# An encoder block: Conv B computed in a third Strassen section of the gate stage, and attention re-paced around a smaller filler

## The chip, the cores and the metric

The kernel runs on one core of one Trainium2 chip. The metric is the device time of one execution in microseconds. The engines are named as in the profile: PE (TensorE, matmuls), DVE (VectorE), ACT (ScalarE), POOL (GpSimd), and SP, which issues most DMAs.

## The reference

One layer, sequence length T = 1024, model width D = 1024, 16 heads of 64, batch 1, everything float32:

```python
h = rmsnorm(x, ln1_g) * (1 + sc1) + sh1          # sc, sh, g from silu(c) @ ada_w + ada_b
q, k, v, cb, cc, cx, ga, gb = split(h @ w_in)    # eight 1024 x 1024 projections
q, k = rmsnorm per head
y_a = stick_breaking_attention(q, k, v)          # 128-query blocks, strictly causal:
      # z = q.k / 8;  a[t,s] = sigmoid(z[t,s]) * prod over s<j<t of (1 - sigmoid(z[t,j]))
y_b = cb * causal_dwconv3(cc * cx)
merged = sigmoid(ga) * (y_a @ w_branch_a) + sigmoid(gb) * (y_b @ w_branch_b)
x = x + g1 * (merged @ w_out)
h = rmsnorm(x, ln2_g) * (1 + sc2) + sh2
x = x + g2 * ((silu(h @ w_ffn_gate) * (h @ w_ffn_up)) @ w_ffn_down)
```

"Conv B" is the projection cb. The change touches it, the attention, and the way to `y_a @ w_branch_a`.

## The kernel before

**Numbers.** Each float32 operand of a matmul is split into a high part, rounded to the fast matmul format by ScalarE (`AF.Copy`), and a low part, the difference, which VectorE computes. A product of two operands takes three matmuls: high by high, high by low, low by high.

**Stages in order of time.** (1) Norm of x, and projections of k and the first half of v. (2) The gate stage: q, Conv C, Conv x and the two branch gates. (3) Attention, with other matmuls as filler. (4) `w_branch_a`, merge, `w_out`. (5) The feed-forward part.

**The gate stage** works by Strassen's method in Winograd's form. A "gate" is one pair (section, j): a 256-column piece of one projection over all of T. `gates` lists them: four of q (section 5), then for j = 0..3 one of Conv C (section 1) and one of Conv x (section 2), then four of each branch gate (4 and 3), 20 in all. For a gate, GpSimd forms four sums of weight blocks (`s1` to `s4`), seven products of 12 matmuls each are computed (`g_prod`, `half_prod`, 128x128 by 128x512), and VectorE combines them into four results of 128x512. `put` says what happens to a result: section 1 is kept, section 2 goes to `put_u`, which multiplies Conv C by Conv x, forms the causal 3-tap convolution y (ScalarE and two VectorE operations) and stores it to `d_y` in DRAM. GpSimd forms the weight sums of the next gate while the present one is on TensorE. Between `put`s, `later()` works off q's remaining steps, and `mods_later` sums the modulation vectors on VectorE during the branch gates.

**Attention** runs over steps s = (head, query tile i), i in `ORDER`, 0 to 7. A step has `att_scores` (z into one or two PSUM banks, sigmoid by ScalarE into a buffer `pt` of 1024 columns, filled from the right), `att_trans` of the tile two steps back (PE transposes of 128x128 blocks, then high part `ath` by ScalarE and low part `atl` by VectorE), `att_scan` of its own tile (on VectorE the running product from the right, in place in `pt`, with the constant `mk` as second input: 128 x 128(i+1)), and at every second step `att_av` for a pair of tiles (matmuls of `vt` by `ath` and `atl` into `o`). The differences of neighbouring rows of v take the place of v in that product: `att_dv` computes vb - va, and splits it into the two halves of `vt`; one matmul therefore gives the high half of v's contribution in rows 0 to 63 of `o` and the low half in rows 64 to 127. ScalarE adds `vlast` to the first half (`otmp`), VectorE adds the second (`oy`), and SP stores the result to `d_ya`.

**The filler** is a generator, `fillers()`, that yields after each small piece of matmuls with a cost written in the code: first the second half of v (two halves `e`, the first of them ahead of attention as `HEAD`), then Conv B as plain product (16 tiles of 128x512, times y from `d_y`, split and stored to `d_yb`), then `w_branch_b` (16 tiles, times the sigmoid gate, stored to `d_mb`). The weights come by `load_ch` (DMA, two splits by `g_split`). The attention steps yield too, with the weights `F_Z`, `F_T`, `F_O`; filler is emitted so that the sum of its costs follows the sum of the steps' weights, except for `TAIL` = 10, which is kept for the last steps, in which only transposes and `att_av` are left.

**What sets the order.** PE's instructions in attention and filler, and VectorE's of attention, are chained in the order in which they are emitted. Other engines' instructions are placed by a scheduler ahead of time, and each engine runs its list in order. `tile(tag, bufs)` gives the next of `bufs` rotating buffers, and waits until its last reader is done.

**After attention** `d_ya` is read back as 16 tiles `yr` of 128x512 (n = half of T, k = pair of heads), split into `ya`, in buffers that attention frees, and multiplied by `w_branch_a`.

## Time and profile before

| | |
|---|---|
| three runs | 1823.03, 1827.53, 1828.09 us; median 1827.53 |
| the profiled execution | 1827.39 us, of which the span from first to last instruction is 1825.6 |
| granted TensorE clock | 0.997 |
| instructions | 24915 |
| DMA | 357.50 MB, mean 196 GB/s |

A row of a group reads: line, engine, operation, tiles, shapes, count, then busy time in us and mean ns of one, then idle time ahead of it with what ended it. A row of a timeline begins with start and length in us. A row of the waits names who waited for whom: us in total, times, longest. A row of busy time by stretches gives the stretch, its length, then busy us and count of instructions for each engine, then the clock, the DMA share and GB/s. L137 is a helper, `tt`, through which many element-wise operations go: those are told apart by their tiles. "PE e", "PE pj" and so on name the PSUM tile that is written. Matmuls overlap, and their recorded length is longer than the time from one start to the next.

### The profile page before, as it was taken

How to read it: one execution, taken by the hardware profiler on the slowest of the kernel's cores; microseconds unless marked ns; L12 is line 12 of the kernel's file. 1: busy time of each engine (PE TensorE's matmuls, PEld its weight loads, DVE VectorE, ACT ScalarE, POOL GpSimd, SP SyncE). 2: the span in 40 equal slices, each digit the busy share in tenths (PEclk: the TensorE clock that was granted, in tenths of full speed). 3: DMA queues.
4: the chain of work that ended last, by engine and by line, in shares of the span. 5: the costliest groups of instructions: out<-in, count | busy, mean ns of one | idle time of the engine just before them, and what ended most of it. 6: DMA issues, size and time to landing. Idle time of an engine off the chain costs nothing.

```text
span 1825.6 us, 24915 instructions
## 1 busy us (share of the span) xinstructions
PE 1799.5 (99%) x8829; PEld 1502.2 (82%) x8829; DVE 1356.8 (74%) x1957; ACT 794.9 (44%) x1494; POOL 368.5 (20%) x277
## 2 busy tenths in 40 slices
PE   7999999999999999999999999999999999999999
PEld 5788778887879988888888788877888888878887
DVE  7873877779872899999887554689977888644776
ACT  3452653333343666666665221663444344322321
POOL 0043328323230000000000000115534544200000
PEclk9999999999999999999999999999999999999999
DMA  9687551227748566689654546324533344299766
GB/s 394 199 319 292 181 184 69 87 84 252 273 152 247 149 180 190 196 222 304 163 141 151 174 162 217 124 88 161 196 149 140 148 166 159 104 363 325 279 230 220
DMA packets 163508, 357.50 MB, mean 196 GB/s; under 512 B 15464, under 2 KB 60848, under 8 KB 161208
## 3 DMA queue, kind: packets, MB, share of 16 engines
q1 hardware_dynamic: 130920, 289.65, 47.5%
q10 hardware_dynamic: 31456, 62.59, 9.5%
q0 software_dynamic: 1008, 3.67, 0.5%
q8 instruction: 71, 1.16, 0.3%
q14 instruction: 53, 0.43, 0.1%
HBM read 245.22 MB, written 110.66 MB: 195 GB/s over the span
## 4 chain that ended last, share of the span: by engine, by line
PE 86%; DVE 7%; DMA 4%; issue 1%; ACT 1%; POOL 0%; SPq 0%; ACTq 0%; DVEq 0%; POOLq 0%
PE e L133 7%; PE e L132 7%; PE e L134 7%; PE pj L134 5%; PE pj L132 5%; PE pj L133 5%; PE pj L309 5%; PE pj L908 5%; PE pj L910 4%; PE pj L909 4%; PE e L1456 4%; PE e L1458 4%; PE e L1457 4%; PE tr L832 3%; PE o L848 2%; PE z L808 2%
## 5 line engine op out<-in xcount | busy, mean ns | idle before, releaser
L818 DVE TENSOR_TENSOR_SCAN pt<-pt,mk 128x128 f32<-128x128 f32 (+7 forms) x128 | 172.4, 1347 | 13.0 <-ACT pt L810 13.0
L132 PE MATMUL e<-big,whi 128*128 128x512 f32 x352 | 137.9, 392 | 2.0 <-DVE c L137 2.0
L133 PE MATMUL e<-big,whi 128*128 128x512 f32 x352 | 137.7, 391 | 0.0
L134 PE MATMUL e<-big,wlo 128*128 128x512 f32 x352 | 137.5, 391 | 0.0
L123 POOL TENSOR_SCALAR rs_m<-ss 128x1 f32<-128x1 f32 x8 | 2.3, 282 | 642.9 <-ACT xn L1259 642.9
L137 DVE TENSOR_TENSOR c<-e,c 128x512 f32<-128x512 f32 x138 | 92.8, 686 | 51.4 <-PE e L134 50.5
L132 PE MATMUL pj<-big,whi 128*128 128x512 f32 x320 | 125.2, 391 | 1.4 <-DVE c L137 1.4
L134 PE MATMUL pj<-big,wlo 128*128 128x512 f32 x320 | 124.8, 390 | 0.0
L133 PE MATMUL pj<-big,whi 128*128 128x512 f32 x320 | 124.6, 389 | 0.0
L1456 PE MATMUL e<-whi,f 128*128 128x512 f32 (+1 forms) x319 | 121.8, 382 | 1.1 <-DMA f<-d_f 1.1
L137 DVE TENSOR_TENSOR c<-pj,c 128x512 f32<-128x512 f32 x140 | 93.0, 681 | 38.9 <-PE pj L134 38.4
L1457 PE MATMUL e<-wlo,f 128*128 128x512 f32 (+1 forms) x319 | 121.8, 382 | 0.0
L1458 PE MATMUL e<-whi,f 128*128 128x512 f32 (+1 forms) x319 | 121.6, 382 | 0.0
L836 DVE TENSOR_TENSOR atl<-tr,ath 128x512 fp32r<-128x512 f32 (+1 forms) x192 | 103.9, 550 | 19.4 <-ACT ath L835 17.9
L810 ACT ACTIVATE pt<-z,rq 128x512 f32<-128x512 f32 (+1 forms) x192 | 104.7, 575 | 26.6 <-PE z L809 26.4
L908 PE MATMUL pj<-big,whi 128*128 128x512 f32 x256 | 114.0, 445 | 0.0
L309 PE MATMUL pj<-whi,big 128*128 128x512 f32 x352 | 109.3, 396 | 3.9 <-ACT big L292 3.9
L137 POOL TENSOR_TENSOR ws<-raw,raw 128x512 f32<-128x512 f32 x40 | 56.3, 1407 | 275.5 <-DMA raw<-w_cg 165.8
L137 DVE TENSOR_TENSOR wlo<-raw,whi 128x512 fp32r<-128x512 f32 x116 | 88.3, 766 | 31.6 <-ACT whi L463 31.0
L463 ACT ACTIVATE whi<-raw 128x512 fp32r<-128x512 f32 x116 | 72.4, 628 | 86.9 <-PE pj L133 45.4
L835 ACT ACTIVATE ath<-tr 128x512 fp32r<-128x512 f32 (+1 forms) x192 | 93.3, 487 | 30.0 <-PE tr L832 29.1
L133 PE MATMUL e<-rl,whi 128*128 128x512 f32 x264 | 102.8, 389 | 1.5 <-DVE rl L137 1.5
(258 smaller groups left out, 4998.6 us busy)
## 6 DMA issues: line engine op xcount, KB each, us to landing
f<-d_f SPq DMA_DIRECT2D x77, 512.0 KB, 4.3
d_f<-fs SPq DMA_DIRECT2D x70, 512.0 KB, 3.2
raw<-w_cg SPq DMA_DIRECT2D x40, 512.0 KB, 3.8
raw<-w_u SPq DMA_DIRECT2D x26, 512.0 KB, 3.2
raw<-w_g SPq DMA_DIRECT2D x25, 512.0 KB, 3.4
ad<-ada ACTq DMA_DIRECT2D x19, 512.0 KB, 4.5
ada<-ada SPq DMA_DIRECT2D x8, 1024.0 KB, 11.6
d_t<-ts SPq DMA_DIRECT2D x16, 512.0 KB, 3.7
```

The costliest lines, as they stand in the source:

```text
L132: nc.tensor.matmul(ps, wh[:, k, :], fh[:, k, :], start=(k == 0), stop=False)
L133: nc.tensor.matmul(ps, wh[:, k, :], fl[:, k, :], start=False, stop=False)
L134: nc.tensor.matmul(ps, wl[:, k, :], fh[:, k, :], start=False, stop=(k == 3))
L137: eng.tensor_tensor(out=out, in0=a, in1=b, op=op)
L309: nc.tensor.matmul(ps, a, b, start=(k == 0 and q == 0), stop=(k == KT - 1 and q == 2))
L810: nc.scalar.activation(pt[:, off + s0:off + s0 + m], z[:, :m], AF.Sigmoid, scale=rq[:, 1, i, h:h + 1])
L818: nc.vector.tensor_tensor_scan(out=pt[:, rev], data0=pt[:, rev], data1=mk[:, rev], initial=1.0, op0=ALU.mult, op1=ALU.max)
L836: nc.vector.tensor_tensor(out=tl[:, :nb, c0:c0 + P], in0=src, in1=th[:, :nb, c0:c0 + P].bitcast(F32), op=ALU.subtract)
L908: nc.tensor.matmul(ps, wh, rh_, start=(k == 0), stop=False)
L1456: nc.tensor.matmul(o, sh, w[0][:, c], start=(j == 0), stop=False)
L1457: nc.tensor.matmul(o, sh, w[1][:, c], start=False, stop=False)
L1458: nc.tensor.matmul(o, sl, w[0][:, c], start=False, stop=(j == NJ - 1))
```

## The change

Conv B leaves the filler and becomes section 0 of the gate stage, after Conv C and Conv x of the same j; 24 gates in all. `put_u` keeps y in an SBUF tile (`ys`) in place of storing it. `put_b`, new, multiplies a result of section 0 by y on GpSimd, splits it on ScalarE and VectorE, and stores both parts to `d_yb` from ScalarE's queue.

In attention the tiles go in the order 6, 7, 0, 1, 4, 5, 2, 3 (the last head in 0 to 7). The transposes come three steps after the scores (lag 3, was 2), `att_av` four steps after (`DAV`, was 3), and there are six `pt` buffers. Filler is placed by a table `FT` of weights for each of the eight steps of a head, all at the end of the transposes; `v` is yielded in pieces of half the size. `att_dv`, from the second head on, and the low parts of the weights of `w_branch_b` move to GpSimd. The two halves of `o` are no longer added by VectorE: ScalarE evacuates all 128 rows (`vlast` has zeros in rows 64 to 127), both halves are stored, and after the load back GpSimd adds them (VectorE for the last pair of heads).

```diff
--- before.py
+++ after.py
@@ -69,10 +69,9 @@
     d_yb = [[drp.tile([P, KT, 512], F32, name=f"d_yb{e}{n}") for n in range(2)] for e in range(2)]
-    d_ya = [drp.tile([P, KT, 512], F32, name=f"d_ya{n}") for n in range(2)]
+    d_ya = [drp.tile([KT, P, 2, 512], F32, name=f"d_ya{n}") for n in range(2)]
     d_sga = drp.tile([KT, P, T], F32, name="d_sga")
     d_sgb = drp.tile([KT, P, T], F32, name="d_sgb")
-    d_y = drp.tile([KT, P, T], F32, name="d_y")
     d_mb = drp.tile([KT, P, T], F32, name="d_mb")
@@ -456,15 +455,15 @@
-    def g_split(src):
+    def g_split(src, eng=nc.vector):
         split_at.append(split_at.pop(0))
...
         nc.scalar.activation(hi, src, AF.Copy)
-        tt(nc.vector, lo, src, hi.bitcast(F32), ALU.subtract)
+        tt(eng, lo, src, hi.bitcast(F32), ALU.subtract)
         return hi, lo
-    gates = ([(5, j) for j in range(4)] + [(sec, j) for j in range(4) for sec in (1, 2)] +
+    gates = ([(5, j) for j in range(4)] + [(sec, j) for j in range(4) for sec in (1, 2, 0)] +
              [(sec, j) for sec in (4, 3) for j in range(4)])
@@ -634,13 +633,24 @@
             raise ValueError(m)
-        y = g_tile()
+        if (m, 0) not in ys and (m, 1) not in ys:
+            yt = gp.tile([P, 2, 512], F32, tag="sq", bufs=2, name=nm("yt"))
+            ys[m, 0], ys[m, 1] = yt[:, 0], yt[:, 1]
+        y = ys[m, n]
         nc.scalar.activation(y, u[:, s + 2:s + 514], AF.Copy, scale=cw[:, m, 2:3])
...
         nc.vector.scalar_tensor_tensor(out=y, in0=u[:, s:s + 512], scalar=cw[:, m, 0:1], in1=y, op0=ALU.mult, op1=ALU.add)
-        nc.scalar.dma_start(d_y[m, :, s:s + 512], y)
-
-    uc = {}
+
+    def put_b(c, m, n):
+
+        hl_ = gp.tile([P, 2, 512], F32R, tag="tr", bufs=2, name=nm("ybt"))
+        tt(nc.gpsimd, c, c, ys[m, n], ALU.mult)
+        nc.scalar.activation(hl_[:, 0], c, AF.Copy)
+        tt(nc.vector, hl_[:, 1], c, hl_[:, 0].bitcast(F32), ALU.subtract)
+        for e in range(2):
+            nc.scalar.dma_start(d_yb[e][n][:, m, :], hl_[:, e].bitcast(F32))
+
+    uc, ys = {}, {}
     pend, pmm, eq = [], [], end_q()
@@ -665,6 +675,8 @@
                 nc.scalar.dma_start((d_sga, d_sgb)[sec - 3][m, :, n * 512:(n + 1) * 512], c)
+            elif sec == 0:
+                put_b(c, m, n)
             elif sec == 1:
@@ -730,10 +742,11 @@
-    NPT = 5
+    NPT = 6
     pts = [ptp.tile([P, D], F32, name=f"pt{j}") for j in range(NPT)]
-    F_Z, F_T, F_O = 0.2,0.3,0
+    FT = ((0.0, 0.0, 0.0, 2.03), (0.0, 0.0, 0.0, 1.17), (0.0, 0.0, 0.0, 0.52), (0.0, 0.0, 0.0, 0.63), (0.0, 0.0, 0.0, 1.66), (0.0, 0.0, 0.0, 0.15), (0.0, 0.0, 0.0, 0.9), (0.0, 0.0, 0.0, 1.45))
+    FT0 = ((0, 1.3, 0, 0), (0, 1.3, 0, 0), (0, .65, .65, 0))
@@ -761,15 +774,15 @@
         if part == 0:
-            tt(nc.vector, dv, dv, va[:, :, cs], ALU.subtract)
+            tt(nc.gpsimd if h else nc.vector, dv, dv, va[:, :, cs], ALU.subtract)
             return
...
         nc.scalar.activation(vt[:, :, :DH], dv, AF.Copy)
-        tt(nc.vector, vt[:, :, DH:], dv, vt[:, :, :DH].bitcast(F32), ALU.subtract)
+        tt(nc.gpsimd if h else nc.vector, vt[:, :, DH:], dv, vt[:, :, :DH].bitcast(F32), ALU.subtract)
...
-        vl = bp.tile([8, 512], F32, tag="vl", bufs=1, name=nm("vl"))
+        vl = fp.tile([P, 512], F32, tag="st", bufs=2, name=nm("vl"))[:8]
         for d, c in (((0, 0),), ((1, 0), (2, 256)))[e]:
@@ -779,9 +792,10 @@
             nc.tensor.transpose(tr[:DH, h * 8:h * 8 + 8], vl[:, h * DH:(h + 1) * DH], ident[:8, :8])
-        nc.scalar.activation(vlast[:, 8 * e:8 * e + 8].rearrange("p h i -> p (h i)"), tr[:DH, :64], AF.Copy)
-
-    vlast = bp.tile([DH, H, 8], F32, name="vlast")
+        nc.scalar.activation(vlast[:DH, 8 * e:8 * e + 8].rearrange("p h i -> p (h i)"), tr[:DH, :64], AF.Copy)
+
+    vlast = bp.tile([P, H, 8], F32, name="vlast")
+    nc.gpsimd.memset(vlast[DH:], 0.0)
     hd, vts, vab = {}, {}, {}
@@ -809,8 +823,8 @@
             if s0 + m < n:
-                yield F_Z
-        yield F_Z
+                yield 0
+        yield 1
@@ -835,7 +849,7 @@
                                     op=ALU.subtract)
-            yield F_T * nb
+            yield 3 - (b0 + 4 < i + 1)
@@ -846,25 +860,25 @@
             lastav[0] = nc.tensor.matmul(o[:, c0:], vt[:, j, :], tl[:, j % 4, c0:], start=False, stop=(j == 2 * g + 1))
-        tmp = bp.tile([DH, 256], F32, tag="otmp", bufs=1, name=nm("otmp"))
-        yv = bp.tile([DH, 256], F32, tag="oy", bufs=3, name=nm("oy"))
+        yv = bp.tile([P, 256], F32, tag="oy", bufs=4, name=nm("oy"))
         for e in range(2):
-            nc.scalar.activation(tmp[:, e * P:(e + 1) * P], o[:DH, e * P:(e + 1) * P], AF.Identity,
+            nc.scalar.activation(yv[:, e * P:(e + 1) * P], o[:, e * P:(e + 1) * P], AF.Identity,
                                  bias=vlast[:, h, 2 * g + e:2 * g + e + 1])
-        nc.vector.tensor_tensor(out=yv, in0=o[DH:], in1=tmp, op=ALU.add)
         hf, c0 = g // 2, (g % 2) * 256
-        nc.sync.dma_start(d_ya[hf][e0:e0 + DH, pr, c0:c0 + 256], yv)
-        yield F_O
-
-    NZ, NTR, NPJ, DAV, KQ = 2, 3, 2, 3, 1
+        for e in range(2):
+            nc.sync.dma_start(d_ya[hf][pr, e0:e0 + DH, e, c0:c0 + 256], yv[e * DH:(e + 1) * DH])
+        yield None
+
+    NZ, NTR, NPJ, DAV, KQ = 2, 3, 2, 4, 1
     LAST = (0, 1, 2, 3, 4, 5, 6, 7)
-    ORDER = (0, 1, 2, 3, 4, 5, 6, 7)
+    ORDER = (6,7,0,1,4,5,2,3)
...
             flush[0] = s >= len(steps)
+            row[0] = (FT0 + FT)[s] if s < len(FT0) else FT[s % 8] if s < len(steps) else ()
             if s < len(steps):
@@ -883,7 +897,7 @@
                 yield from att_scores(h, i)
-            tr_ = att_trans(*steps[s - 2]) if 0 <= s - 2 < len(steps) else iter(())
+            tr_ = att_trans(*steps[s - 3]) if 0 <= s - 3 < len(steps) else iter(())
             av_ = att_av(steps[s - DAV][0], steps[s - DAV][1] // 2) if s >= DAV and s % 2 != DAV % 2 else iter(())
@@ -896,9 +910,9 @@
-    def load_ch(src):
+    def load_ch(src, eng=nc.vector):
         raw = g_raw(src)
-        return g_split(raw[:, :512]), g_split(raw[:, 512:])
+        return g_split(raw[:, :512], eng), g_split(raw[:, 512:], eng)
@@ -920,41 +934,21 @@
                 for k in range(KT):
-                    if k == 4:
-                        yield 1.3
+                    if k in (2, 4, 6):
+                        yield 0.65
                     wh, wl = (v[:, (k % 2) * 256:(k % 2) * 256 + 256] for v in w[k // 2])
...
                 if i % 2 == 0:
-                    v2 = fq.tile([P, 512], F32, tag=("ybh", "ybl")[i // 2 % 2], bufs=2, name=nm("vs1"))
+                    v2 = fq.tile([P, 512], F32, tag="ybh", bufs=2, name=nm("vs1"))
                 vs = v2[:, i % 2 * 256:i % 2 * 256 + 256]
...
                     put_before(1 + e)
-                yield 1.3
-        cb_w = {}
-        for m, n in [(m, n) for m in range(KT - 2) for n in range(2)] + [(m, n) for n in range(2) for m in (KT - 2, KT - 1)]:
-            if n == 0:
-                cb_w[m] = load_ch(w_cg[0, m])
-            w = cb_w[m]
-            y = fp.tile([P, 512], F32, tag="st", bufs=3, name=nm("cy"))
-            nc.sync.dma_start(y, d_y[m, :, n * 512:(n + 1) * 512])
-            ps = ps_f()
-            for kk in range(0, KT, KQ):
-                if kk:
-                    yield 0.65 * KQ
-                mm_ch(ps, w, hh[n], hl[n], kk, kk + KQ)
-            nc.vector.tensor_tensor(out=y, in0=ps, in1=y, op=ALU.mult)
-            yh = fq.tile([P, 512], F32R, tag="ybh", bufs=2, name=nm("ybh"))
-            yl = fq.tile([P, 512], F32R, tag="ybl", bufs=2, name=nm("ybl"))
-            nc.scalar.activation(yh, y, AF.Copy)
-            nc.vector.tensor_tensor(out=yl, in0=y, in1=yh.bitcast(F32), op=ALU.subtract)
-            nc.sync.dma_start(d_yb[0][n][:, m, :], yh.bitcast(F32))
-            nc.sync.dma_start(d_yb[1][n][:, m, :], yl.bitcast(F32))
-            yield 0.65 * KQ
+                yield 0.65
         def load_sb(m, n):
@@ -971,22 +965,22 @@
             if n == 0:
-                wb[m] = load_ch(w_b[m])
+                wb[m] = load_ch(w_b[m], nc.gpsimd)
             sb = sbs.pop(0) if sbs else load_sb(m, n)
...
                 mm_ch(ps, wb[m], yh[n], yl[n], kk, kk + KQ)
-            mb = fp.tile([P, 512], F32, tag="st", bufs=3, name=nm("mb"))
+            mb = fp.tile([P, 512], F32, tag="st", bufs=2, name=nm("mb"))
             nc.vector.tensor_tensor(out=mb, in0=ps, in1=sb, op=ALU.mult)
...
-    FILL = 2.5 * 16 * 5.2
-    ATT = sum(F_Z * (1 + i // 4) + F_T * (i + 1) + F_O * (i % 2) for i in range(8)) * H
-    HEAD, TAIL = 16, 10.0
-    FILL -= 1.3 * HEAD
+    FILL = 1.5 * 16 * 5.2
+    ATT = sum(sum(r) for r in FT) * H + sum(sum(a) - sum(b) for a, b in zip(FT0, FT))
+    HEAD, TAIL = 32, 10.0
+    FILL -= 0.65 * HEAD
     fl = fillers()
@@ -1008,16 +1002,16 @@
     at_ = attention()
-    flush, nfl = [0], 0
+    flush, nfl, row = [0], 0, [()]
     pe, mine = len(nc.cur_bb.bb.instructions), set()
...
         with tc.high_priority():
-            ca_ = next(at_, None)
+            ca_ = next(at_, -1)
         mine.update(i.name for i in nc.cur_bb.bb.instructions[n0:])
-        if ca_ is None:
+        if ca_ == -1:
             break
-        ta += ca_
+        ta += row[0][ca_] if ca_ is not None and row[0] else 0
         nfl += flush[0]
@@ -1058,8 +1052,10 @@
             for k in range(KT):
-                yr = fp.tile([P, 512], F32, tag="yr", bufs=2, name=nm("yr"))
-                nc.sync.dma_start(yr, d_ya[n][:, k, :])
+                yr2 = fp.tile([P, 2, 512], F32, tag="yr", bufs=2, name=nm("yr"))
+                nc.sync.dma_start(yr2, d_ya[n][k])
+                yr = yr2[:, 0]
+                tt(nc.vector if k == KT - 1 else nc.gpsimd, yr, yr, yr2[:, 1], ALU.add)
                 tag, bufs = slots[n * KT + k]
...
```

2 lines of the change are left out of this document (1 added, 1 removed).

## The prediction

> **What bounds the kernel now.** I read the page first, then the busy time by stretches, then TensorE's waits in attention, then the timelines of one gate and one head.
>
> ```profile
> PE 1799.5 (99%) x8829; PEld 1502.2 (82%) x8829; DVE 1356.8 (74%) x1957; ACT 794.9 (44%) x1494; POOL 368.5 (20%) x277
> ```
> ```profile
> core 0: us, PE busy (x) PEld busy (x) DVE busy (x) ACT busy (x) POOL busy (x), PEclk, DMA share, GB/s
> 200.00:400.00 200.00, 200.00 (x884) 161.99 (x883) 151.53 (x214) 81.25 (x136) 91.47 (x60) 1.00 0.33 115
> 400.00:450.00 50.00, 48.65 (x214) 39.85 (x214) 48.24 (x68) 16.29 (x27) 15.87 (x8) 1.00 0.65 226
> ...
> 600.00:700.00 100.00, 99.91 (x683) 91.00 (x682) 86.82 (x122) 65.72 (x154) 0.00 (x0) 1.00 0.64 165
> 700.00:800.00 100.00, 100.00 (x613) 87.30 (x612) 91.37 (x130) 65.92 (x151) 0.00 (x0) 1.00 0.66 185
> 800.00:900.00 100.00, 100.00 (x607) 87.41 (x606) 89.57 (x127) 65.40 (x146) 0.00 (x0) 1.00 0.84 247
> ```
> ```profile
> PE z L808 <- ACT pt L810: 0.4, 2, 0.2
> PE tr L832 <- DVE pt L818: 0.2, 1, 0.2
> ```
> The gate stage (200 to 400 us is inside it) and attention (600 to 900) are both full on TensorE at clock 1.00; the waits listed for its matmuls in 575 to 985 us come to 0.6 us (last fence). VectorE is second: 76% busy in the gates and 267.8 of 300 us, 89%, in attention, where GpSimd does nothing. So first of all a matmul costs its issue interval wherever it stands, and the question is whether TensorE stays the bound when a fifth of its attention work has gone.
>
> **Matmuls removed and added.** The profile's 390 ns for one is not its price, since they overlap; starts are.
>
> ```profile
> 544.69 0.39 PE L132 MATMUL pj<-big,whi 128*128 128x512 f32 x1
> ...
> 550.13 0.39 PE L132 MATMUL pj<-big,whi 128*128 128x512 f32 x1
> ```
> ```profile
> 759.69 0.40 PE L908 MATMUL pj<-big,whi 128*128 128x512 f32 x1
> 759.92 0.39 PE L909 MATMUL pj<-big,whi 128*128 128x512 f32 x1
> 760.15 0.39 PE L910 MATMUL pj<-big,wlo 128*128 128x512 f32 x1
> 760.38 0.28 PE L847 MATMUL o<-ath,vt 128*128 128x256 f32 x1
> ```
> In the gates 24 matmuls lie between the two rows: 5.44 / 24 = 0.2267 us each. In attention three fillers take 0.69 us, 0.230 each. Conv B as filler is 16 tiles of 8 k-slices and 3 matmuls, 384: **-88.3 us** (-87.1 at the gates' rate). As a third section it is 4 gates of 7 products of 12, 336: 336 x 0.2267 = **+76.2 us**. That is -12.1, from 48 matmuls that the seven-product form saves.
>
> **The rest of the gate stage.** Each of the four new gates lasts 84 x 0.2267 = 19.0 us. VectorE gets 7 sums, 7 low halves and 4 of put_b's, 18 operations of 0.7 to 0.8 us, some 14 us; GpSimd four weight sums and four products. Neither fills the 19 us. GpSimd's products wait for results of the running gate, and the next gate's weight sums may be queued behind them:
>
> ```profile
> 353.66 1.75 POOL L137 TENSOR_TENSOR ws<-raw,ws 128x512 f32<-128x512 f32 x1
> ...
> 371.73 0.39 PE L132 MATMUL pj<-ft,whi 128*128 128x512 f32 x1
> ```
> The sum in the first row is used by the product that starts in the second, 18 us later, so a queue of a few microseconds is hidden. If the sums fell behind the gate's last product, cover would be the next gate's first two products, 5.4 us, against 0.7 (sum on VectorE), three GpSimd operations of 1.3 and 1.3 to split, 5.9 and some latency: about 1 us in each of 4 gates. On the other side, TensorE lost 1.35 us in 400 to 450, where VectorE was 96% full; four put_u move ahead of that place. Bounds -1.4 to +4, taken 0, nearest to the full row of 200 to 400. The eight 512 KB weight loads and the stores of y move into a stage whose DMA share is 0.33: nothing, as the y stores (16) and their reloads go altogether.
>
> **Attention: does TensorE stay the bound?**
>
> ```profile
> 608.95 2.28 DVE L818 TENSOR_TENSOR_SCAN pt<-pt,mk 128x1024 f32<-128x1024 f32 x1
> ...
> 983.28 2.28 DVE L818 TENSOR_TENSOR_SCAN pt<-pt,mk 128x1024 f32<-128x1024 f32 x1
> ```
> ```profile
> L818 DVE TENSOR_TENSOR_SCAN pt<-pt,mk 128x128 f32<-128x128 f32 (+7 forms) x128 | 172.4, 1347 | 13.0 <-ACT pt L810 13.0
> L836 DVE TENSOR_TENSOR atl<-tr,ath 128x512 fp32r<-128x512 f32 (+2 forms) x188 | 101.3, 548 | 19.0 <-ACT ath L835 17.5
> L854 DVE TENSOR_TENSOR oy<-o,otmp 64x256 f32<-64x256 f32 x62 | 26.4, 426 | 16.8 <-ACT otmp L852 15.5
> L137 DVE TENSOR_TENSOR wlo<-raw,whi 128x512 fp32r<-128x512 f32 x36 | 24.2, 679 | 10.0 <-ACT whi L463 9.4 <-PE tr L832 0.5
> L950 DVE TENSOR_TENSOR cy<-pj,cy 128x512 f32<-128x512 f32 x16 | 10.9, 681 | 2.2 <-PE pj L910 2.0
> L954 DVE TENSOR_TENSOR ybl<-cy,ybh 128x512 fp32r<-128x512 f32 x16 | 10.8, 675 | 0.1
> L953 ACT ACTIVATE ybh<-cy 128x512 fp32r<-128x512 f32 x16 | 10.1, 631 | 10.8 <-DVE cy L950 9.0 <-DMA skl<-d_k 1.8
> L137 DVE TENSOR_TENSOR vb<-vb,va 128x512 f32<-128x512 f32 x16 | 10.8, 672 | 0.8 <-DMA vb<-d_v 0.8
> L137 DVE TENSOR_TENSOR vt<-vb,vt 128x512 fp32r<-128x512 f32 x16 | 10.7, 671 | 0.0
> ```
> From scan to scan of the last tile there are 15 heads: 374.3 / 15 = 24.96 us a head. Without 24 fillers it is 24.96 - 5.5 = **19.4 us**, if TensorE never waits. VectorE has 0.893 x 24.96 = 22.3 us in a head now. It loses, per head: four oy, 4 x 0.426 = 1.7; one cy and one ybl, 1.4; vb and vt (15 of 16 heads), 1.3; two weight halves, 1.4. That leaves **16.5 us, 85% of 19.4**. In busy shares the change keeps the balance that was there. ScalarE is no nearer: 0.66 x 24.96 = 16.5 us, less ybh and one half of conv B's weights (0.63 each), is 15.2 of 19.4, 78%.
>
> What moves to GpSimd is vb, vt and the halves of w_b: three operations in a head. They are not free for VectorE:
>
> ```profile
> 337.84 1.29 POOL L137 TENSOR_TENSOR ws<-raw,raw 128x512 f32<-128x512 f32 x1 [12.28 <-DVE gt L640]
> 339.08 1.75 POOL L137 TENSOR_TENSOR ws<-raw 128x512 f32<-128x512 f32 x1
> 340.80 1.29 POOL L137 TENSOR_TENSOR ws<-raw,ws 128x512 f32<-128x512 f32 x1
> ```
> ```profile
> 338.30 1.38 DVE L137 TENSOR_TENSOR wlo<-raw,whi 128x512 fp32r<-128x512 f32 x1
> 339.60 1.28 DVE L137 TENSOR_TENSOR c<-pj,c 128x512 f32<-128x512 f32 x2
> ...
> 346.94 0.67 DVE L137 TENSOR_TENSOR wlo<-raw,whi 128x512 fp32r<-128x512 f32 x1
> ```
> The subtraction of two SBUF tensors that started at 338.30 took 1.38 us instead of 0.67: it ended 0.6 us after GpSimd's operation did. GpSimd's next took 1.75 instead of 1.29. The two sums at 339.60, with one input in PSUM, ran at full speed meanwhile. So such operations go one after the other. [...]
>
> The scan reads pt and mk, both SBUF, so I assume that it waits as well. Bounds: 0 to 3 x 1.29 = 3.9 us of VectorE waiting per head. GpSimd gets in when a scan ends; then VectorE has one or two atl (0.55 us in the mean, PSUM input) ahead of its next scan, which hide that much: some 0.45 us an operation, 1.4 in a head. VectorE is then at 17.9 us, 92%. At no wait the sum is that of full TensorE; at 3.9 VectorE needs 20.4 us, 1.0 over, +16 us in 16 heads.
>
> The lag of three helps: a scan has two whole steps until its transposes, 2 x 19.4 / 8 = 4.9 us, where it had one of 24.96 / 8 = 3.1; the longest atl and scan together take 1.4 + 2.3. The order 6, 7, 0, 1, 4, 5, 2, 3 puts short tiles behind long ones, with filler weighted to the long. The sigmoid's wait, the o bank and the six pt buffers keep a step or more of slack. Loads of q, k and v have the head's 19.4 us instead of 25. The stores of yv, now two each (64 more issues on SP), replace 16 loads of y, 32 stores of y_b halves and 8 weight loads there: nothing; each waits for ScalarE alone where it waited for oy on VectorE, so the loads queued behind it on SP go no later. At attention's start the order puts the long tiles 6 and 7 first, under filler of 1.3 units a step as before; taken 0. For the waits, and local stalls where GpSimd lands ahead of a long scan, I take **+3** of 0 to +16.
>
> **Attention's end.**
>
> ```profile
> 1006.95 0.39 PE L910 MATMUL pj<-ya,wlo 128*128 128x512 f32 x1
> 1009.04 0.47 PE L908 MATMUL pj<-ya,whi 128*128 128x512 f32 x1 [1.71 <-DVE mb L982]
> ```
> ```profile
> 988.37 3.33 DMA yr<-d_ya
> 993.52 7.06 DMA raw<-w_o
> ```
> Here TensorE stood still 1.7 us for a bank that mb frees, and mb stood on VectorE behind splits of ya. There the chain of waits goes through yr loads (3.3 us), two buffers deep, and a 7 us load of w_o that held ScalarE. Each yr now is twice as large and has a GpSimd sum (1.3 us) before its split, two abreast: up to 1 us more a tile for some six tiles after the last o, behind 48 matmuls (10.9 us) of tiles that need only the first half. A sum that waits for its load also holds the w_b halves queued behind it on GpSimd, and with them filler. The drain is one step longer, under the same 10 units of filler. Bounds -1.7 (the stall goes) to +6, taken **+1**, nearer to the present stall.
>
> **Sum.** The profiled run took 1827.4 us (span 1825.6), the median of the runs is 1827.5. 1827.4 - 88.3 + 76.2 + 0 + 3 + 1 = **1819 us**, 0.5% less. About 0.3%, 5.5 us, can be told from no change: faster is below 1822.0, slower above 1833.0.
>
> **Rivals.** First, slower: GpSimd's lock makes VectorE the bound of attention. For it: the row at 338.30, scans being 10.8 us of each head, and that no row shows TensorE full with VectorE above 91.4%. If VectorE can fill no more than the 89% that it fills now, TensorE waits as soon as 16.5 plus waits pass 0.893 x 19.4 = 17.3, at 0.8 us a head; each further microsecond adds 16 / 0.893 = 18 us, so 1.8 us a head (0.6 per GpSimd operation) is the point from which the kernel is slower than before. Half of the full wait, 1.95 us, gives +20, **1836**; all of it 1871. Against it: the longer lag, atl between scans, and that 89% was no limit, as nothing waited there. [...] 0.28.
>
> Second, no change to be measured: the waits are as I think, but the gate queue (+4), the end (+6) and stalls of 5 us all come: 1827.4 - 12.1 + 4 + 6 + 5 = **1830**. 0.14.
>
> Third, that seven products don't save 48 matmuls: excluded, the loops fix the counts.
>
> **How the numbers follow.** Forecast, TensorE the bound in both stages: 0.58, its own range 1808 to 1822 (the terms at 1827.4 - 12.1 - 1.4 - 1.7 = 1812, and the runs of before reach 4 us under their median). Up to 1840 comes the gain eaten and the rival at a little over half of its wait; above lies a tenth. Faster 0.58, same 0.14, slower 0.28.
>
> **What would show it.** Right: gates longer by 76 us at 84 matmuls in 19.0; heads of 19.4 us from long scan to long scan; TensorE's waits in attention of a few us; scans beside GpSimd lengthened by up to 1.3. Wrong: heads of 20.5 or more, transposes waiting for scans, or `o` for atl; a product waiting for whi of ws in the new gates; matmuls waiting over 5 us for ya or mb.

## The result, and the profile after

The changed kernel takes 1840.47 us (median of 4 runs, 1837.32 to 1843.25), the kernel before, run beside it, 1825.74: a ratio of **1.0081, interval 1.0057 to 1.0105**. Forecast were 1819 us and a range of 1808 to 1840. It is slower where faster was forecast.

The profiled execution took 1839.56 us (span 1837.8, granted clock 0.994), before 1827.39 (1825.6, 0.997). The engines by the page of the profile, then four stretches (the columns are TensorE, its weight loads, VectorE, ScalarE, GpSimd, then clock, DMA share and GB/s):

```profile
PE 1794.8 (98%) x8781; PEld 1498.1 (82%) x8781; DVE 1351.1 (74%) x1873; ACT 794.0 (43%) x1510; POOL 519.5 (28%) x370
```
```profile
200.00:400.00 200.00, 200.00 (x885) 162.02 (x884) 153.88 (x207) 83.08 (x141) 105.29 (x68) 1.00 0.32 108
...
500.00:600.00 100.00, 91.10 (x395) 72.97 (x394) 87.97 (x137) 35.95 (x61) 30.51 (x18) 0.98 0.75 255
...
700.00:800.00 100.00, 97.27 (x688) 89.24 (x687) 85.24 (x103) 72.14 (x176) 31.03 (x17) 1.00 0.92 249
800.00:900.00 100.00, 99.27 (x661) 89.14 (x661) 89.51 (x108) 71.91 (x175) 29.93 (x18) 1.00 0.75 194
```
TensorE has its 48 matmuls less and is still the fullest engine, but no longer full: 97.27 and 99.27 of 100 us in attention, where it had 100.00, and 91.10 at the end of the gate stage. VectorE is at 87% in attention (174.75 of 200 us), not above the 91.37 that it had. What TensorE waited for, in attention (660 to 1040 us), then in the gates:

```profile
PE pj L941 <- ACT vs L947: 2.4, 1, 2.4
PE tr L846 <- DVE atl L850: 2.2, 5, 0.9
PE z L822 <- ACT pt L824: 1.8, 1, 1.8
PE o L862 <- DVE atl L850: 1.4, 4, 0.6
PE pj L922 <- ACT ya L1062: 1.3, 1, 1.3
PE z L822 <- DMA skh<-d_k: 1.3, 1, 1.3
```
```profile
PE pj L133 <- DVE wlo L136: 4.8, 2, 2.7
PE pj L131 <- DVE c L136: 3.6, 4, 1.8
PE pj L131 <- ACT whi L462: 0.5, 1, 0.5
```
No engine is a new bound. There are single waits of 1 to 3 us, each of another kind. And some of them cost more than their length. Here is the stretch around one of them, the product at 594.58 that waited 2.10 us for a low half:

```profile
594.58 0.50 PE L133 MATMUL pj<-ft,wlo 128*128 128x512 f32 x1 [2.10 <-DVE wlo L136]
```
```profile
592.00:595.00 3.00, 0.90 (x4) 0.42 (x4) 3.00 (x4) 1.86 (x4) 0.83 (x1) 1.00 0.40 114
595.00:596.00 1.00, 1.00 (x5) 0.79 (x4) 1.00 (x3) 0.64 (x1) 0.00 (x0) 0.81 0.96 387
596.00:599.00 3.00, 3.00 (x8) 2.30 (x7) 2.22 (x6) 2.18 (x4) 0.00 (x0) 0.50 0.80 269
599.00:602.00 3.00, 3.00 (x14) 2.46 (x13) 1.28 (x2) 0.00 (x0) 1.82 (x2) 0.99 0.26 100
```
The third column from the end is the granted clock. One us after the wait it falls to 0.50 for 3.41 us (595.62 to 599.04): 8 matmuls start in 3 us instead of 14. That is 1.7 us lost, with TensorE recorded as busy. The same follows the 2.43 us gap at 670 (0.50 at 671 to 674) and the 1.83 us gap at 935.84 (0.50 at 937 to 940).

**Where the time went.** The table divides each span at the end of the modulation's last matmuls (end of the gate stage) and at the first matmul of `w_out`. "Idle" is the time between recorded matmuls (in the first column from 165 us on, where the gate stage begins), "clock" is the sum of (1 - granted clock) over stretches of 10 us.

| us | gate stage ends | idle, clock | attention and Conv A | idle, clock | rest of span | idle, clock |
|---|---|---|---|---|---|---|
| before | 566.1 | 3.4, 1.7 | 524.7 | 2.5, 0.0 | 734.8 | 4.7, 1.7 |
| sum of the matmul terms | 642.3 | | 436.4 | | 734.8 | |
| after | 649.2 | 8.9, 1.7 | 450.2 | 11.3, 3.4 | 738.4 | 6.4, 3.4 |

After lies 6.9, 13.8 and 3.6 us over the matmul terms. Idle time accounts for 5.5 + 8.8 + 1.7 = 16.0, the clock for 0 + 3.4 + 1.7 = 5.1, and 3.2 are in neither and stay unexplained. So -12.1 became +12.2.

One profile is one execution, and the clock varies between executions. Over several runs the difference is larger: before has 0.9990 on average in 23 runs (beside a later version), 1.8 us of clock lost in an execution, and 0.9985 to 0.9991 beside the others; after has 0.994, 0.994, 0.995, 0.994, which is 10.6 us. Of the 14.7 us between the medians, some 8 to 9 are clock.

### The profile page after: what moved, and what is told of

It is laid out like the page before. It is cut to its first block, busy times and chain, and to the rows that moved or that the text cites. A ratio compares the mean times of both kernels' runs of the same rounds, so it can differ in the third digit from the quotient of the medians.

```text
span 1837.8 us, 24714 instructions
## 1 busy us (share of the span) xinstructions
PE 1794.8 (98%) x8781; PEld 1498.1 (82%) x8781; DVE 1351.1 (74%) x1873; ACT 794.0 (43%) x1510; POOL 519.5 (28%) x370
## 4 chain that ended last, share of the span: by engine, by line
PE 72%; DVE 12%; DMA 7%; ACT 4%; issue 3%; POOL 1%; SPq 0%; ACTq 0%; DVEq 0%; POOLq 0%
PE e L133 6%; PE e L131 6%; PE e L132 6%; PE pj L131 6%; PE pj L133 6%; PE pj L132 6%; PE pj L308 5%; PE e L1452 4%; PE e L1454 4%; PE e L1453 4%; PE tr L846 2%; PE pj L922 2%; PE pj L923 2%; PE pj L924 2%; PE o L862 2%
## 5 line engine op out<-in xcount | busy, mean ns | idle before, releaser
L832 DVE TENSOR_TENSOR_SCAN pt<-pt,mk 128x896 f32<-128x896 f32 (+7 forms) x128 | 188.3, 1471 | 15.7 <-ACT pt L824 15.7
L131 PE MATMUL pj<-big,whi 128*128 128x512 f32 x384 | 150.5, 392 | 3.6 <-DVE c L136 3.6
L133 PE MATMUL pj<-big,wlo 128*128 128x512 f32 x384 | 149.8, 390 | 0.0
L132 PE MATMUL pj<-big,whi 128*128 128x512 f32 x384 | 149.5, 389 | 0.0
L136 POOL TENSOR_TENSOR ws<-raw,raw 128x512 f32<-128x512 f32 x44 | 61.4, 1395 | 292.0 <-DMA raw<-w_cg 173.8
L136 DVE TENSOR_TENSOR c<-pj,c 128x512 f32<-128x512 f32 x168 | 111.8, 681 | 43.2 <-PE pj L133 42.9
L850 DVE TENSOR_TENSOR atl<-tr,ath 128x512 fp32r<-128x512 f32 (+1 forms) x192 | 99.3, 543 | 32.9 <-ACT ath L849 32.5
L133 PE MATMUL pj<-ft,wlo 128*128 128x512 f32 x288 | 112.5, 392 | 4.8 <-DVE wlo L136 4.8
L131 PE MATMUL pj<-ft,whi 128*128 128x512 f32 x288 | 112.9, 392 | 0.5 <-ACT whi L462 0.5
L132 PE MATMUL pj<-ft,whi 128*128 128x512 f32 x288 | 112.8, 392 | 0.0
L462 ACT ACTIVATE whi<-ws 128x512 fp32r<-128x512 f32 x96 | 58.4, 626 | 110.5 <-POOL ws L136 65.1
```

What stands on the lines that cost most here:

```text
L131: nc.tensor.matmul(ps, wh[:, k, :], fh[:, k, :], start=(k == 0), stop=False)
L132: nc.tensor.matmul(ps, wh[:, k, :], fl[:, k, :], start=False, stop=False)
L133: nc.tensor.matmul(ps, wl[:, k, :], fh[:, k, :], start=False, stop=(k == 3))
L136: eng.tensor_tensor(out=out, in0=a, in1=b, op=op)
L462: nc.scalar.activation(hi, src, AF.Copy)
L832: nc.vector.tensor_tensor_scan(out=pt[:, rev], data0=pt[:, rev], data1=mk[:, rev], initial=1.0, op0=ALU.mult, op1=ALU.max)
```

## The experiments

All ratios are against the kernel before, run beside the version on the same chip. My theory was that buffers and queues, which the change shares out anew, make the waits; the rival, the prediction's first, that GpSimd's "lock" on VectorE does. The word stands there for what the prediction's row at 338.30 shows, a subtraction on VectorE that took 1.38 us instead of 0.67 beside GpSimd's operations; the runs show how much longer operations get, not by what mechanism. V and Q in the later expectations are VectorE's chain of scans against single queues and transfers.

### The change in two parts

`move_only`: the kernel before, with Conv B's move and `put_b` alone; attention as before.

```diff
-    gates = ([(5, j) for j in range(4)] + [(sec, j) for j in range(4) for sec in (1, 2)] +
+    gates = ([(5, j) for j in range(4)] + [(sec, j) for j in range(4) for sec in (1, 2, 0)] +
...
+            elif sec == 0:
+                put_b(c, m, n)
...
-    FILL = 2.5 * 16 * 5.2
+    FILL = 1.5 * 16 * 5.2
```

> The kernel before with Conv B moved to the gate stage and nothing else changed: lag 2, order 0 to 7, halves of o added by VectorE, v's differences and w_b's halves on VectorE, no GpSimd operation in attention. VectorE's need per head is 22.3 - 1.4 (cy, ybl) - 0.7 (one half of conv B's weights) = 20.2 us against 19.4 for TensorE. Theory A: VectorE becomes the bound, heads of 20.2 us or more (22 if it can be filled to 91% only), +13 to +45 us over full TensorE: 1.00 to 1.02, so the re-pacing of the changed kernel pays for itself. Theory B (GpSimd's lock is what costs): no lock here, scans stay at 172 us in total, heads at or under those of the changed kernel (19.9 us), 1.00 or less.

`pace_only`: the new attention, with Conv B still as its filler and, for room, five `pt` buffers.

```diff
-    gates = ([(5, j) for j in range(4)] + [(sec, j) for j in range(4) for sec in (1, 2, 0)] +
+    gates = ([(5, j) for j in range(4)] + [(sec, j) for j in range(4) for sec in (1, 2)] +
...
-    NPT = 6
+    NPT = 5
...
+        cb_w = {}
+        for m, n in [(m, n) for m in range(KT - 2) for n in range(2)] + [(m, n) for n in range(2) for m in (KT - 2, KT - 1)]:
...
-    FILL = 1.5 * 16 * 5.2
+    FILL = 2.5 * 16 * 5.2
```

> The changed kernel with Conv B back in attention's filler (so 20 gates, and filler of 25 us heads), but all else of the new attention kept: lag 3, new order, GpSimd for v's differences, w_b's halves and the sums after the load; five pt buffers, as before, for room. Theory A: single stalls of the new attention remain (v's evacuation 4 us, queue order on GpSimd and ScalarE 3 to 4 us): 1.002 to 1.005. Theory B: GpSimd lengthens scans by some 16 us as in the changed kernel, but heads of 25 us hide it: 0.998 to 1.001.

The move alone takes 1852.52 us, **1.0159 (1.0143 to 1.0176)**, the pacing alone 1833.06, **1.0038 (1.0024 to 1.0052)**. With the move alone attention lasts 467.0 us and TensorE waits in it so:

```profile
PE tr L843 <- DVE pt L829: 14.3, 30, 0.9
PE o L859 <- DVE atl L847: 2.4, 6, 0.9
PE tr L843 <- DVE atl L847: 1.7, 2, 0.9
```
Thirty times transposes wait for a scan: with the filler gone, the old pacing is too tight. In the changed kernel that row is gone, as the prediction's working of the lag said; on top of the move the new attention brings the ratio from 1.0159 to 1.0081. Which part of it does so isn't shown: the lag, the order, the placing of filler and the operations taken off VectorE change together. But it isn't free: with the old amount of filler it costs 0.4%. There scans take 188.6 us in all, as after (188.3, before 172.4), and no transpose or `o` waits: the prolonged scans are hidden. Its one long wait is 3.7 us for `vs`, at 587 us; attention's idle time is 5.9 us, 3.4 more than before, and the clock of 584 to 594 us is 0.66, 3.4 us lost. So most of its loss in attention is that of a buffer, which comes next. (Its rest of the span is 2.4 us longer than before's too, after a gap of 3.56 us at 1255.95.)

### Two shared buffers

The wait at 670.55 comes from this:

```profile
670.12 0.66 ACT L947 ACTIVATE vs<-pj 128x256 f32<-128x256 f32 x2 [3.19 <-DMA d_v<-vs]
```
ScalarE's evacuation of a piece of v waits until the store of an earlier piece has left its buffer. `fillers()` had four tiles of two pieces each for them, in the tags `ybh` and `ybl`; the change drops `ybl`, and two tiles are left. `pace_only` has the same two. The other edit concerns the gate stage: `put_b` takes its buffers from the tag `tr`, which the modulation's loads rotate through as well, and stores them from ScalarE's queue:

```profile
494.12 0.63 ACT L462 ACTIVATE whi<-raw 128x512 fp32r<-128x512 f32 x1 [6.09 <-DMA d_yb<-ybt]
...
495.56 1.30 POOL L136 TENSOR_TENSOR ws<-raw,raw 128x512 f32<-128x512 f32 x1 [9.20 <-ACT whi L462]
...
508.43 0.50 PE L133 MATMUL pj<-ft,wlo 128*128 128x512 f32 x1 [2.74 <-DVE wlo L136]
```
Two loads queued on ScalarE, `cab` and a row of the modulation (`ad`), had to wait until `put_b`'s stores had left the two buffers; they were issued at 489.23 and 493.73. Behind them stood a weight's high half, for 6.09 us, and behind that GpSimd's weight sums. The same late `cab` holds up VectorE's modulation sums, which stand in its queue ahead of low halves. A product waits for one of those 13 us on. `g_t`, below, shows which of the two ways counts.

`vs_yr`: v's pieces in the two `yr` buffers that attention's end uses, eight pieces again.

```diff
-                if i % 2 == 0:
-                    v2 = fq.tile([P, 512], F32, tag="ybh", bufs=2, name=nm("vs1"))
+                if i % 4 == 0:
+                    v2 = fp.tile([P, 1024], F32, tag="yr", bufs=2, name=nm("vs1"))
...
```

> The changed kernel with one edit: the evacuations of v's second half (line L947 of the changed kernel) use two buffers of four quarters, which the end of attention uses later, where they had two buffers of two. Theory A (the forecast's mechanism holds, TensorE is the bound, and the 20 us over the forecast are single stalls with a slower clock after the longer ones): the 2.4 us gap at 670 us (matmul waiting for ACT vs) goes, and the 1.7 us that the clock of 0.83 costs behind it: attention 4 us shorter, 12 instead of 15 us over the kernel before, 1.006 instead of 1.008. Theory B (GpSimd's operations lengthen the scans, VectorE is late, TensorE waits in every head): no gain in total, since the heads set the time; 1.008.

`g_t`: the last `put_b` before the modulation starts, in the tag `t`.

```diff
+        if (m, n) == (3, 1):
+            hl_ = [gp.tile([P, 512], F32R, tag="t", bufs=2, name=nm("ybt")) for e in range(2)]
...
```

> The changed kernel with one edit: in the last gate of section 0 one of put_b's four pairs of tiles comes from the tag t, so that the load of cab and of the first modulation rows, which use the tag tr too, no longer wait for the last stores of y_b. Theory A: ScalarE's queue stood 6 us behind those DMA issues at 488 to 494 us; without it the gate stage loses no more than it did before (3.4 us of gaps instead of 8.9): 5 us less, 1.005. Rival: the gaps at 508 to 595 us come from VectorE, 93% busy there with the modulation sums and the late start is not their cause: no change, 1.008.

`gv` has both.

> Both edits of the first pair together (v's evacuations in the two buffers of the end, one pair of put_b's tiles in the tag t). Theory A: the parts add, as they are in different stages: gates to 642 us, attention and w_branch_a 446 to 447, the rest 735: span 1824, 1.000 to 1.002 of the kernel before. Theory B (VectorE and GpSimd's lock set attention): the same here for the gates, but attention stays at 450: 1.003.

Measured: `vs_yr` 1833.04 us, **1.0047 (1.0032 to 1.0062)**, the wait for `vs` gone and attention 446.7 us; `g_t` 1832.47, **1.0040 (1.0024 to 1.0056)**; `gv` 1830.31, **1.0028 (1.0015 to 1.0041)**. In `g_t` the gates' longest waits shrink:

```profile
PE pj L133 <- DVE wlo L136: 3.4, 2, 2.1
PE pj L131 <- DVE c L136: 0.8, 2, 0.5
PE pj L131 <- ACT whi L462: 0.4, 1, 0.4
```
The way to that product shows in `cab`'s first use on VectorE, in after and then in `g_t`:

```profile
497.15 2.04 DVE L136 TENSOR_TENSOR cab<-cab,uu 128x1024 f32<-128x1024 f32 x1 [1.08 <-ACT uu L546]
```
```profile
493.52 1.23 DVE L136 TENSOR_TENSOR cab<-cab,uu 128x1024 f32<-128x1024 f32 x1 [5.03 <-ACT uu L546]
```
It starts 3.6 us earlier in `g_t`, and the product's wait falls from 2.74 to 1.35 us. The high half comes only 0.7 us earlier there (493.39) and GpSimd's sums come later (496.93 instead of 495.56), so it is VectorE's queue that counts here rather than GpSimd's.

`g_t`'s gate stage ends at 642.5 us, as the matmul term says, but in the nine later kernels with the same gate stage (`mods_late`, below, is not one of them) it ends at 644.4 to 647.3, and with the unedited one at 647.5 to 649.2 (three kernels): the edit is worth some 3 us of the 6.9. Two buffer tags thus carry about two thirds of the loss against before, 1.0081 to 1.0028. (The two edits alone save 0.34 and 0.41%, together 0.53; the intervals leave open whether they add.)

### Is it GpSimd's lock?

Three kernels, all `gv` with GpSimd's new attention work back on VectorE: the low halves of `w_b` (`gv_wb`), the differences of v (`gv_dv`), both (`gv_all`). The first two pairs of lines are `gv_dv`'s, the third is `gv_wb`'s.

```diff
-            tt(nc.gpsimd if h else nc.vector, dv, dv, va[:, :, cs], ALU.subtract)
+            tt(nc.vector, dv, dv, va[:, :, cs], ALU.subtract)
-        tt(nc.gpsimd if h else nc.vector, vt[:, :, DH:], dv, vt[:, :, :DH].bitcast(F32), ALU.subtract)
+        tt(nc.vector, vt[:, :, DH:], dv, vt[:, :, :DH].bitcast(F32), ALU.subtract)
-                wb[m] = load_ch(w_b[m], nc.gpsimd)
+                wb[m] = load_ch(w_b[m])
```

> As the kernel with both edits, and the low halves of w_b's weights back on VectorE; GpSimd keeps v's differences. Theory A: two operations a head lock VectorE out instead of three (scans some 181 us in total), VectorE has 0.7 us more a head (17.2 of 19.4), and v's differences no longer stand behind w_b's halves in GpSimd's queue, so the wait of z for a sigmoid at 929 us (1.7 us, and as much by the clock) goes: attention 3 us shorter, 0.998 to 1.000. Theory B: 16 halves more on VectorE and 21 us less of GpSimd: the scans' saving is larger, attention 5 us shorter or more.

> As the kernel with both edits, and v's differences back on VectorE; GpSimd keeps w_b's halves. Theory A: scans some 177 us in total, VectorE 17.8 us a head before waits; the wait for a sigmoid goes as well: attention 2 to 3 us shorter, 0.998 to 1.001. Theory B: 5 us shorter or more.

> As the kernel with both edits, and nothing on GpSimd during attention but the sums after the load. Scans at 172 to 174 us. Theory A: VectorE needs 16.5 + 2.7 = 19.2 us of a head of 19.4 and can't be filled that far, so transposes and o wait in every head: attention 455 us or more, 1.004 or more. Theory B: GpSimd's lock was the cost (16 us of longer scans), so this one is the fastest: attention under 443, 0.997 or less.

`gv_wb` 1.0037 (1.0023 to 1.0051), `gv_dv` 1.0035 (1.0023 to 1.0048), `gv_all` **1.0036 (1.0023 to 1.0049)**: none differs from `gv`. The scans do become shorter; `gv_all`'s row of the page, and its waits in attention:

```profile
L836 DVE TENSOR_TENSOR_SCAN pt<-pt,mk 128x896 f32<-128x896 f32 (+7 forms) x128 | 175.8, 1373 | 15.2 <-ACT pt L828 15.2
```
```profile
PE o L866 <- DVE atl L854: 5.1, 9, 1.2
PE tr L850 <- DVE atl L854: 2.3, 4, 0.9
```
175.8 us of scans instead of 188.8 in `gv`. In exchange the waits for `atl` are 7.4 us (`gv`: 3.1), as VectorE has three more operations a head. So the scans do lose time beside GpSimd, but moving these operations back gains nothing: they fill VectorE instead, and the time is the same. The price of the longer scans by itself isn't shown, as no version leaves these operations out; `no_scan`, next, bounds the part that goes through the scans. That VectorE so full would keep attention at 455 us or more fell too: it is 447.7.

### What is left

`gv` still has 450.7 us in attention, 14 over the sum, 10.4 of them idle and 5.1 clock (its profiled execution took 1834.51 us, 4 over its median):

```profile
PE o L865 <- ACT ath L853: 2.4, 1, 2.4
PE pj L926 <- ACT ya L1066: 2.3, 1, 2.3
PE tr L850 <- DVE atl L854: 1.9, 5, 0.7
PE o L866 <- DVE atl L854: 1.2, 2, 1.0
PE z L826 <- DMA skh<-d_k: 1.1, 1, 1.1
```
Three kernels on `gv`: `no_scan` (scans cut to the last 128 columns of each tile, so it leaves out work that the result needs), `late_y` (half of y_b's loads only when `w_branch_b`'s tile (1,0) starts; the expectation calls it Conv B's), `tail_vec` (all sums of output halves on VectorE).

```diff
no_scan
-        rev = slice(D - 1, off - 1 if off else None, -1)
+        rev = slice(D - 1, D - P - 1, -1)
late_y
+        def load_y(n):
...
+        load_y(0)
...
+            if m == 1 and n == 0:
+                load_y(1)
tail_vec
-                tt(nc.vector if k == KT - 1 else nc.gpsimd, yr, yr, yr2[:, 1], ALU.add)
+                tt(nc.vector, yr, yr, yr2[:, 1], ALU.add)
```

> The kernel with both edits of storage (the v buffers of four quarters, the last gate output of section 0 in its own tag), and the scan of every attention tile cut to the tile's last 128 columns: the scan of the other columns is left out, so about 95 us of VectorE's 189 us of scans go, some 7 us a head, and what VectorE holds under its lock against GpSimd goes with it. Theory V (VectorE's chain scan - transposes - atl is what still keeps attention at 447 to 451 us instead of 436): the waits of o for atl go and attention with Conv A falls to 437 to 442 us, the time to 0.993 to 0.999 of the kernel before. Theory Q (the rest is in queues and transfers that the scan has no part in: skh behind y_b's loads, ya at the end, the clock that falls after each longer gap): attention with Conv A stays at 446 to 450 us and the time at 1.001 to 1.004.

> The kernel with both edits of storage, and the loads of y_b's second half (8 transfers of 512 KB) issued only once Conv B's tile (1,0) starts, instead of all 16 together. Theory Q: SP's queue has skh's and skl's loads behind those transfers at 749 to 757 us; with them moved, the gaps before z and o at about 766 to 771 us (3.5 us in that kernel, 1.1 to 2.4 us in its sisters) go, and the granted clock no longer falls at 770 us; attention with Conv A 446 to 449 us instead of 450.7, the time 1.001 to 1.003 of the kernel before. Theory V: the gaps are where VectorE is late anyway; the time stays at 1.0028, within 0.001.

> The kernel with both edits of storage, and all 16 sums of attention's output halves (yr) on VectorE, where the change has only the two of k = 7 there. If GpSimd's sums are what Conv A waits for at attention's end, the gap before Conv A's matmul at about 1022 us (2.3 us, waiting for ya) falls below 1.5 us and the time by 0.5 to 1.5 us, to 1.002 to 1.0025 of the kernel before. If VectorE is what is late there, 14 more sums of about 0.35 to 0.7 us on it make the gap longer or bring waits for atl in the last heads, and the time goes to 1.003 to 1.005. If neither, it stays at 1.0028, within 0.001.

`no_scan`: 1827.13 us, **1.0017 (1.0003 to 1.0030)**, attention 443.3, between the two theories, with the time in Q's range. The waits for `atl` fall from 3.1 to 1.1 us and idle time from 10.4 to 5.9:

```profile
PE pj L926 <- ACT ya L1066: 1.9, 2, 1.1
PE z L826 <- DMA d_mb<-mb: 1.5, 1, 1.5
PE tr L850 <- DVE atl L854: 0.9, 1, 0.9
```
So VectorE's chain holds between 2.0 us of attention's idle time, what the waits for `atl` lost, and 4.5, all that went; 1.7 of the rest is one wait for `ath`, which is absent in `late_y` too, with whole scans. The wait for `ya` stays, and the one for `d_mb` is new. Of the 7.4 us by which attention is shorter, 1.7 are clock, and in time the intervals of `gv` and `no_scan` overlap. What the scans that GpSimd lengthens cost attention is a part of this.

`late_y`: 1829.29, 1.0024 (1.0014 to 1.0033), attention 445.6. The wait for `skh` or `skl` is still there, 1.1 us; `gv`'s clock loss at 770 is absent (770 to 780 us: 1.00, in `gv` 0.76). Against `gv` the time is the same within the intervals, so that these loads are its cause isn't shown.

`tail_vec`: 1837.9, **1.0075 (1.0063 to 1.0087)**. The gap before Conv A is 1.1 us instead of 2.3, as one branch of the expectation had it, and two far longer ones came, at 730 and 775. The first on VectorE and on TensorE:

```profile
728.80 0.76 DVE L136 TENSOR_TENSOR yr<-yr 128x512 f32<-128x512 f32 x1 [6.08 <-DMA d_ya<-oy]
```
```profile
730.21 0.48 PE L850 MATMUL tr<-dm,pt 128*128 128x128 f32 x1 [5.46 <-DVE atl L854]
```
A sum whose data isn't there stands at the head of VectorE's queue for 6.08 us, with `atl` and scans behind it. In `gv`, with the sum on GpSimd, no such gap stands there, although a sum takes 1.29 us on GpSimd and 0.69 on VectorE (medians). So what the change gains by these sums on GpSimd is not a matter of their duration, but of the queue that waits.

`combo`: `late_y` with the halves of `w_b` (the expectation says Conv B's) on VectorE and the last four sums too.

```diff
-                wb[m] = load_ch(w_b[m], nc.gpsimd)
+                wb[m] = load_ch(w_b[m])
-                tt(nc.vector if k == KT - 1 else nc.gpsimd, yr, yr, yr2[:, 1], ALU.add)
+                tt(nc.vector if k == KT - 1 or n == 1 and k > 3 else nc.gpsimd, yr, yr, yr2[:, 1], ALU.add)
```

> The kernel with both edits of storage and the later loads of y_b, and two edits more that take single waits away: the low halves of Conv B's weights on VectorE (in the run that did it alone the gap before z, where ScalarE had waited for GpSimd's v difference, was gone), and the last four of the 16 sums of attention's output halves on VectorE, after its last scan. Theory Q (attention's excess is a number of single waits in queues and the clock lost after them): the gaps of 1.7 us before z at 927 us and of 1.5 us at Conv A's start shrink or go, attention with Conv A 442 to 445 us, the time 1.000 to 1.002 of the kernel before. Theory V (VectorE's chain sets attention's pace): 16 more subtractions and 4 sums on VectorE make the waits for atl longer by what they save elsewhere; attention with Conv A stays at 445 to 448 us and the time at 1.0024, within 0.001. Neither expects it under 0.998.

1831.05, **1.0033 (1.0020 to 1.0047)**: the wait at 927 us is gone, attention is 447.5, and the waits for `atl` have grown from 3.4 to 7.4 us. Theory V was right here: what was moved to VectorE came back as waits.

`no_scan_late` has both edits, `no_scan` and `late_y`, and leaves out the same work as `no_scan`; `mods_late` is `late_y` with the modulation's steps shifted from the first two of the last eight gates to later ones.

```diff
mods_late
-        for _ in range((5 if sec in (3, 4) else 0) if g + 1 < len(gates) else 50):
+        for _ in range(((3, 3, 5, 6, 6, 6, 6)[g - 16] if sec in (3, 4) else 0) if g + 1 < len(gates) else 50):
```

> The kernel with both edits of storage and the later loads of y_b, with the scans cut to the last 128 columns of each tile: the scan of the other columns is left out. If queues and scans are two causes that add up (450.7 us without either, 445.6 with the later loads, 443.3 with the cut scans), attention with Conv A falls to 436 to 440 us, the idle time of TensorE in it to 2 to 4 us, and the time to 0.997 to 1.000 of the kernel before. If the two edits took away the same waits, the stage stays at 442 to 445 us and a third cause is open; the time is then 1.0005 to 1.003.

> The kernel with both edits of storage and the later loads of y_b; in the gate stage's last two sections the 35 steps of the modulation (a load on ScalarE's queue and a product on VectorE each) go 3, 3, 5, 6, 6, 6, 6 to the seven gates instead of 5 to each. If they are what the gates wait for at 586 and 592 us (gaps of 2.0 and 1.2 us, then 10 us at a clock of 0.83), these gaps go, the gate stage ends at 642 to 643.5 us instead of 645.3, and the time is 1.000 to 1.0015 of the kernel before; the two gaps at 507 and 522 us stay. If the gaps come from the gates' own weight loads, they stay and the stage ends at 645 to 646 us, the time at 1.0024 within 0.001.

`no_scan_late`: 1826.97, **1.0007 (0.9995 to 1.0020)**, attention 442.0. It didn't come down to the sum. Its longest waits are `skh` (2.7 us) and `ya` at the end (1.4), which neither edit removes; and its clock is 0.9964 on average in 10 runs, 6.6 us lost against 1.8 before. Without that difference, 4.8 us, it would be 2.9 us faster than before. `mods_late`: 1829.29, 1.0024 (1.0015 to 1.0034), gate stage to 646.8 us, with a gap of 3.49 us at 587.52. So this sharing of the steps doesn't remove the gap, which lies in the second gate of the last section; but it is a weak test, as 23 of the 35 steps still stand ahead of that gate where there were 25. Before has a gap in the same place (2.09 us at 511.45). Its cause stays open.

No version beat the kernel before.

## Why the prediction was wrong

**Right: the price of the matmuls.** Take idle and clock away, and attention with Conv A is 522.2 us before; less 88.3 it is 433.9. In after it is 450.2 - 11.3 - 3.4 = 435.5, in `no_scan` 434.0, in `late_y` 436.7. The gate stage, so reduced, grew by 77.6 us against 76.2. Seven products did save 48 matmuls, and the 12.1 us are there.

**Right: that scans take longer beside GpSimd, and that this doesn't make VectorE the bound.** Scans went from 172.4 to 188.3 us, 1.0 us a head where 1.4 of waiting was estimated. The first rival, which had the sign right, was wrong in its size: by its sum the kernel is slower than before only from 1.8 us of waiting a head on. Its signs were there, but small: `o` waited 1.4 us for `atl` and transposes 2.2 us in the whole of attention. `gv_all`, with the waiting mostly gone, is as slow as `gv`, though it has the moved work on VectorE.

**Wrong: "the rest of the gate stage", 0, with +4 as its end.** It was +6.9. The step that failed is the cover of the edits costed at nothing. The prediction followed GpSimd's queue, which is hidden as said, but for `put_b` it counted only operations: not the rotation of its buffers with the modulation's, which makes VectorE's sums late and with them the low halves. `g_t` takes some 3 of the 6.9 us away; the rest of them stays open.

**Wrong: "+3" for attention's waits.** With the end of attention, +13.8 stands against +4 together. The long scans show a head:

```profile
681.32 2.29 DVE L832 TENSOR_TENSOR_SCAN pt<-pt,mk 128x1024 f32<-128x1024 f32 x1 [1.58 <-ACT pt L824]
...
960.28 2.28 DVE L832 TENSOR_TENSOR_SCAN pt<-pt,mk 128x1024 f32<-128x1024 f32 x1
```
(960.28 - 681.32) / 14 = 19.93 us, not 19.4, still below the 20.5 that was named as proof of the rival. The bound of +16 held, the value was taken too near its lower end, and from a count of busy shares. At equal shares a shorter head leaves each chain less time in us. Idle time by causes, from the experiments: one wait of 2.4 us for v's buffers, gone in `vs_yr` (where the stage's idle time is 1.7 lower), 2.0 to 4.5 by VectorE's chain (`no_scan` against `gv`), the rest in single queues. One of these is the chain behind the gap at 935.84, GpSimd's queue first:

```profile
917.68 3.18 POOL L136 TENSOR_TENSOR wlo<-raw,whi 128x512 fp32r<-128x512 f32 x1 [4.48 <-ACT whi L462]
922.86 1.28 POOL L136 TENSOR_TENSOR vt<-vb,vt 128x512 fp32r<-128x512 f32 x1 [1.99 <-ACT vt L780]
...
930.57 3.46 POOL L136 TENSOR_TENSOR vb<-vb,va 128x512 f32<-128x512 f32 x2 [6.43 <-issue]
```
```profile
934.06 0.63 ACT L1062 ACTIVATE ya<-yr 128x512 fp32r<-128x512 f32 x1 [3.24 <-POOL vb L136]
934.60 0.61 ACT L865 ACTIVATE oy<-o,vlast 128x128 f32<-128x128 f32 x2
935.10 1.16 ACT L824 ACTIVATE pt<-z,rq 128x512 f32<-128x512 f32 x2
```
A half of `w_b` waits on GpSimd for ScalarE and takes 3.18 us; the half of `vt` comes after it, and the next differences of v (`vb`) another 6.43 us later. ScalarE's `ya` goes into a buffer of v that these differences still read, and waits 3.24 us for them, with `oy` and the sigmoids behind it. The prediction named the sums that hold `w_b`'s halves, not the halves that hold v. In `gv_wb` and `combo`, with these halves on VectorE, the gap isn't there. But in `g_t` and `gv`, with the halves on GpSimd, it is only 0.52 us, so the start of this chain, the halves, isn't shown to be its cause.

**Wrong: "+1" for attention's end.** Conv A's wait for `ya` is 1.3 us (1.1 to 2.5 in the versions made from after), with 1.7 before for `mb`: inside -1.7 to +6, no cause of the loss.

**Missing: the clock after a wait.** The sum has no term for it, though the trace of before shows it: in 510 to 520 us the granted clock was 0.83, after the 2.09 us gap:

```profile
512.00:515.00 3.00, 3.00 (x9) 2.35 (x8) 3.00 (x6) 2.31 (x5) 0.00 (x0) 0.53 0.75 245
515.00:518.00 3.00, 3.00 (x14) 2.42 (x13) 1.36 (x3) 0.57 (x2) 0.81 (x1) 0.90 0.54 209
```
Waits of about 2 us were counted at their length, and some of them cost 1.7 us more (3.41 us at 0.50); the last section lists them. By the runs' clocks this is some 8 to 9 us of the miss. The second rival's "stalls of 5 us" could have cost nearly twice as much, by an estimate from those 1.7 us a wait.

**Left open.** The rest of the span is 3.6 us longer in after's profile: two waits of 2.48 and 1.99 us at the start of the feed-forward part, where before has 1.45 and 2.01, and their clock. In `gv` and the versions made from it the rest is 734.3 to 736.1, near 734.8, so it varies from one execution or version to the next. What delays `skh` by 1 to 2.7 us isn't settled either.
